# Behind the last store of a decoder layer: 46 ways of reading the streamed tokens on TensorE

## The chip, the cores and the metric

The kernel runs on one core of one Trainium2 chip. The time is device microseconds of that core for one execution of the whole program; a run's median is compared with the median of the kernel before on the same chip. The profile is of one execution, and its span runs from the first to the last recorded instruction.

## The reference

One layer of a hybrid decoder is computed for 256 prompt tokens and 8 sample tokens (264 in all) of width 2048, in float32:

```python
def rmsnorm(x, g):
    xf = x.astype(jnp.float32)
    y = xf * lax.rsqrt(jnp.mean(xf * xf, axis=-1, keepdims=True) + EPS)
    return (y * g.astype(jnp.float32)).astype(x.dtype)
...
    x = x + jnp.concatenate([y_rg, y_ml], axis=-1) @ w_out       # RG-LRU and mLSTM groups
...
    x = x + o @ w_xa_o                                           # cross-attention
    xf = rmsnorm(x, g_ffn)
    x = x + (jax.nn.silu(xf @ w_ffn_gate) * (xf @ w_ffn_up)) @ w_ffn_down
...
    y_prompt = rmsnorm(xp, g_final)
    y_sample = rmsnorm(xs, g_final)
```

The outputs are `y` of all tokens and the new states and memory keys and values.

## The kernel before

Activations are held transposed: features lie on the 128 partitions, tokens along the free dimension. So a product streams the 264 tokens as the moving operand of TensorE past 128x128 blocks of a weight matrix as the stationary one. Each float32 number is split into a rounded part and a rest, both in float32r, and `mm3` (line 232) multiplies with three matmuls: high by high, high by low, low by high.

The work is a list `steps`: each step loads one 128x2048 piece of a weight matrix from memory (two halves of 128x1024, tag `raw`), splits it with ScalarE and VectorE into tiles of the tag `w` (4 buffers of `WW` = 2176 columns), and runs its matmuls into one PSUM bank of `bank()` (line 288, tag `mm`, 4 buffers). Inside a `w` tile the blocks lie 264 columns apart from column 48 on (`wrows`, line 214). The tokens lie in tiles of `Arr` (line 121): four chunks of 264 tokens behind one another in a tile of `BW` = 1088 columns, from column 0 or, in every second tile, from column 32. All matmuls of the kernel stream such tokens, or weights, with a step of one column.

The order of the instructions on SyncE is the program's; the other engines' order comes from the scheduler of the framework, which simulates a timeline. Other work (recurrences, attention) is done by generators between the steps.

The end of the program: `final(m)` (line 930) takes the 16 pieces of the last product, adds them into `xres` and writes the scaled rows to `st["y"]`, four `Arr` tiles of four chunks each. After the last one `rstd_fin` (line 375) works out the reciprocal root of the mean square. A loop at the very end multiplies the 16 chunks of `st["y"]` in place (line 1344: chunks 4, 5, 10 and 11 on GpSimd, the others on VectorE) and stores them in 9 transfers to `o_y` from the queues of SyncE and ScalarE (line 1345). `warm(n)` (line 293) is a helper that runs matmuls into a bank that nobody reads.

Of the kernel before, what the change touches and what calls it, by code (L numbers as in the profile page):

```python
# [11 lines left out]
F32R = mybir.dt.float32r  # L12
I32 = mybir.dt.int32
AF = mybir.ActivationFunctionType
# [3 lines left out]
P = 128  # L18
# [4 lines left out]
N = T + NS  # L23
# [57 lines left out]
def layer_kernel(ctx: ExitStack, tc, xT, memT, vec, wrg, w_in, w_out, w_q, w_k, w_v, w_o,  # L81
                 w_gu, w_d0, w_d1, w_d2, c0T, kcT, vcT,
                 o_y, o_h, o_cp, o_cs, o_pc, o_sc, o_sn, o_m, o_k, o_v):
    nc = tc.nc
    act, dve, pe = Engine(nc.scalar, price_act), Engine(nc.vector, price_dve), Engine(nc.tensor, price_pe)
# [3 lines left out]
    sb = ctx.enter_context(tc.tile_pool(name="sb", bufs=1))  # L89
# [29 lines left out]
    WO, WW = 48, 8 * N + 64  # L119
# [119 lines left out]
    st = {}  # L239
# [18 lines left out]
    def side(g, prio=0):  # L258
        x = Gen(g, prio)
        gens.append(x)  # L260
        gens.sort(key=lambda q: q.prio)
        return x
# [43 lines left out]
    def V(name, j=0, w=1):  # L306
        o = _V[name][0] + j
        return vecs[:, o: o + w]
# [52 lines left out]
    def sumsq(acc, x, first):  # L361
        if first:
            return act.activation(acc, x, AF.Square)
        s = tmp(x.shape[-1])
        i = act.activation(s, x, AF.Square)
        dve.tensor_add(acc, acc, s)
        return i

    def split(h, l, x, g):

        act.activation(h, x, AF.Copy, scale=g)
        dve.scalar_tensor_tensor(l, x, g, h.bitcast(F32), op0=OP.mult, op1=OP.subtract)
# [536 lines left out]

    def residual(m, gname, key, last):

        def f(ps):
            x = xres[:, m, :]
            dve.tensor_add(x, x, ps[:, :N])
            if key is None:
                return
            if m == 0:
                st[key] = HL(KC)  # L920
            split(*st[key](m), x, V(gname, m))
            sumsq(acc_x, x, m == 0)
            if m == KC - 1:
                st["rstd_" + key] = side(last(), -1)
        return f
# [56 lines left out]
    for m in range(KC):  # L982
        proj(w_out[m], ry, residual(m, "g_xa", "xa", norm_x),
             need=("rgout",) if m == 0 else ())
# [23 lines left out]
    pairs = []  # L1008
# [213 lines left out]
    def evac_xo(m):  # L1222
        f = residual(m, "g_ffn", "ffn", norm_x)

        def g(ps):
            if m == 0:
                return
            if m == 1:
                residual(0, "g_ffn", "ffn", norm_x)(held[0][0])
            f(ps)  # L1230
        return g
# [109 lines left out]
    for lo, hi in ((0, 1), (1, 2), (2, 4), (4, 6), (6, 8), (8, 10), (10, 12), (12, 14), (14, 16)):  # L1341
# [2 lines left out]
            e.tensor_mul(st["y"](c), st["y"](c), r)  # L1344
        (act if lo in (1, 4, 8, 12) else sp).dma_start(o_y[:, lo:hi, :], st["y"].tile(lo // 4)[:, lo % 4: lo % 4 + hi - lo, :])


# [1 line left out]
_OUTS = [("o_y", (P, KC, N)), ("o_h", (P, RGB, 1 + NS)), ("o_cp", (P, RGB, 3)), ("o_cs", (P, RGB, NS, 3)),  # L1349
# [102 lines left out]
```

## Time and profile before

| what | value |
|---|---|
| median of 2 runs | 1552.89 us |
| the 2 runs | 1550.15 and 1555.63 us |
| span of the profiled execution | 1548.1 us |
| busy TensorE matmuls | 1533.5 us, 12098 records |
| busy weight loads | 1500.4 us, 12098 records |
| busy VectorE, ScalarE, GpSimd | 1055.5, 784.0, 123.7 us |
| mean granted TensorE clock | 0.997 |

The page gives no total time of the profiled execution beside its span of 1548.1 us; the two runs lie 2.0 and 7.5 us above that span. Times are from the span's start. The recorded length of a matmul includes its way through the pipeline, so matmuls overlap in the records: their rate is read from a count over a stretch of time, not from the length of one.

### The profile page before, as it was taken

Reading aid. Unit: us, or ns where it says so; the run is one execution under the profiler, and the core shown is the slowest. Engines: PE = TensorE matmul, PEld = TensorE weight load, DVE = VectorE, ACT = ScalarE, POOL = GpSimd, SP = SyncE. Lnnn points to the kernel's source line nnn. Section 1 sums busy time; section 2 is a strip of 40 time slices with the busy share of each in tenths; the row PEclk is TensorE's granted clock in tenths of the full one; section 3 lists DMA queues with packets and bytes.
Section 4 is the critical chain, followed back from the end, with each engine's and each line's share of the span. In section 5 each row is a group of like instructions: output and inputs, shape, how many; then the busy total and the mean of one; then the engine's idle time right before and its main releaser. Section 6 shows DMA issues by size and latency. Waiting matters only on the chain.

```text
span 1548.1 us, 30188 instructions
## 1 busy us (share of the span) xinstructions
PE 1533.5 (99%) x12098; PEld 1500.4 (97%) x12098; DVE 1055.5 (68%) x2026; ACT 784.0 (51%) x1255; POOL 123.7 (8%) x190
## 2 busy tenths in 40 slices
PE   9999999999999999999999999999999999999997
PEld 9999999999999888899999999999999999999997
DVE  7886888796699989876665555445555545555554
ACT  7565775665455656555444444333444433444463
POOL 0001210000134333310000000000000000000000
PEclk9999999999999999999999999999999999999999
DMA  9556984547789887855555555555555555555563
GB/s 301 187 164 204 309 288 171 193 158 259 251 294 356 320 296 252 309 181 180 187 177 181 186 181 188 181 185 183 183 185 181 186 183 186 180 188 178 163 181 107
DMA packets 99757, 326.01 MB, mean 211 GB/s; under 512 B 10945, under 2 KB 19825, under 8 KB 99617
## 3 DMA queue, kind: packets, MB, share of 16 engines
q1 hardware_dynamic: 83472, 269.57, 52.1%
q0 software_dynamic: 15136, 53.16, 9.7%
q8 instruction: 94, 1.54, 0.4%
q10 hardware_dynamic: 1008, 1.36, 0.3%
q14 instruction: 47, 0.38, 0.1%
HBM read 312.78 MB, written 11.28 MB: 209 GB/s over the span
## 4 chain that ended last, share of the span: by engine, by line
PE 96%; DVE 2%; ACT 1%; DMA 0%; issue 0%; SPq 0%; DVEq 0%; ACTq 0%
PE mm L60 90%; PE ax L60 6%; DVE B L60 1%; ACT B L60 0%; DVE w L60 0%; DMA raw<-w_in 0%; ACT w L60 0%; ACT L60 0%; DVE xres L60 0%; DVE c L60 0%; ACT rstd L60 0%; SPq L1278 0%; DVE acc_x L60 0%; DVEq L1429 0%; ACT t L60 0%
## 5 line engine op out<-in xcount | busy, mean ns | idle before, releaser
L60 PE MATMUL mm<-B,w 128*128 128x264 f32 (+1 forms) x10960 | 1365.3, 285 | 4.1 <-DVE w L60 2.4
L60 PEld LDWEIGHTS mm<-B,w 128*128 128x128 f32 x10960 | 1338.6, 188 | 16.4 <-DVE w L60 2.8
L60 ACT ACTIVATE w<-raw 128x1024 fp32r<-128x1024 f32 (+1 forms) x522 | 537.9, 1031 | 654.6 <-PE mm L60 447.3
L60 DVE TENSOR_TENSOR w<-raw,w 128x1024 fp32r<-128x1024 f32 (+1 forms) x522 | 623.1, 1195 | 357.0 <-ACT w L60 356.0
L60 PE MATMUL mm<-w,B 128*128 128x512 f32 x384 | 91.0, 391 | 0.0
L60 PEld LDWEIGHTS mm<-w,B 128*128 128x128 f32 x384 | 70.7, 188 | 14.3
L60 DVE TENSOR_TENSOR t<-mm,rstd 128x264 f32<-128x264 f32 x104 | 44.8, 431 | 44.2 <-PE mm L60 43.5
L1344 POOL TENSOR_TENSOR B<-B,rstd 128x264 f32<-128x264 f32 x4 | 2.8, 736 | 855.5 <-ACT rstd L60 855.5
L60 DVE TENSOR_TENSOR xres<-xres,mm 128x264 f32<-128x264 f32 (+1 forms) x81 | 34.2, 423 | 38.9 <-PE mm L60 38.9
L60 DVE SCALAR_TENSOR_TENSOR B<-B,dw 128x256 f32<-128x256 f32 x128 | 55.6, 488 | 3.9 <-ACT dw L60 3.9
L60 DVE SCALAR_TENSOR_TENSOR dw<-B,qsm,dw 128x256 f32<-128x256 f32 x96 | 49.6, 525 | 0.4
L60 PE MATMUL ax<-B,B 128*128 128x256 f32 (+3 forms) x288 | 48.1, 308 | 0.0
L60 PEld LDWEIGHTS ax<-B,B 128*128 128x128 f32 x288 | 40.8, 190 | 3.2 <-ACT w L60 0.3
L1031 POOL TENSOR_TENSOR ds<-dw,ds 128x256 fp32r<-128x256 f32 x32 | 34.6, 1085 | 108.1 <-ACT ds L60 108.1
L60 ACT ACTIVATE B<-xres,vecs 128x264 fp32r<-128x264 f32 (+1 forms) x64 | 32.1, 502 | 1.5 <-DVE xres L60 1.0
L60 ACT ACTIVATE t<-xres 128x264 f32<-128x264 f32 (+2 forms) x61 | 24.0, 410 | 15.2 <-DVE xres L60 15.2
L1020 POOL DMA_DIRECT2D B<-kcT x32 | 17.3, 542 | 140.1 <-DVE B L60 131.0
L60 ACT ACTIVATE B<-t 128x264 fp32r<-128x264 f32 (+1 forms) x60 | 24.2, 409 | 4.6 <-DVE t L60 4.3
L60 DVE TENSOR_TENSOR acc_x<-acc_x,t 128x264 f32<-128x264 f32 x59 | 25.1, 426 | 1.0 <-ACT t L60 0.5
L60 DVE SCALAR_TENSOR_TENSOR B<-xres,vecs,B 128x264 fp32r<-128x264 f32 x48 | 23.4, 487 | 3.1 <-ACT B L60 3.1
L60 ACT ACTIVATE t<-t 128x264 f32<-128x264 f32 (+1 forms) x61 | 24.8, 406 | 1.3 <-DVE t L60 1.2
L60 ACT ACTIVATE dw<-B,qsm 128x256 f32<-128x256 f32 x32 | 16.2, 507 | 17.4 <-DVE B L60 10.7
(152 smaller groups left out, 666.9 us busy)
## 6 DMA issues: line engine op xcount, KB each, us to landing
raw<-w_gu SPq DMA_DIRECT2D x176, 512.0 KB, 3.5
raw<-w_d SPq DMA_DIRECT2D x80, 512.0 KB, 3.5
raw<-w_in SPq DMA_DIRECT2D x74, 512.0 KB, 4.6
raw<-w_out SPq DMA_DIRECT2D x32, 512.0 KB, 4.0
B<-kcT POOLq DMA_DIRECT2D x32, 512.0 KB, 8.1
raw<-w_q SPq DMA_DIRECT2D x32, 512.0 KB, 3.7
B<-vcT POOLq DMA_DIRECT2D x32, 512.0 KB, 8.5
raw<-w_k SPq DMA_DIRECT2D x32, 512.0 KB, 6.8
```

Of the source, the lines that this page charges most:

```text
L60: return f(*a, **k)
L1020: pool_e.dma_start(kc, kcT[h, b])
L1031: pool_e.tensor_sub(ws[:, 1], acc, ws[:, 0].bitcast(F32))
L1344: e.tensor_mul(st["y"](c), st["y"](c), r)
```

## The change

A function `probes` is called after the loop with the last stores. It takes three tiles of the tag `w` and has ScalarE fill them with copies of tiles 0, 1 and 2 of `st["y"]` (six copies of 1056 columns, three of 64). Then 46 access patterns follow, each with 24 matmuls: the stationary operand is a block of 128 columns of the first tile, taken in turn from 8 places 264 columns apart; the moving operand is the pattern's view of the second tile, in float32r. The 24 matmuls add up in one bank; the output is written to columns that lie next to one another, whatever the pattern. Nothing reads the bank, and the third tile isn't read either. TensorE's order in this part is the program's.

A pattern is a start column and a list of [step, count], the outermost first. So "pairs 132 apart" streams columns 0, 132, 1, 133, 2, ..., and "step 4" streams 0, 4, 8, ... 37 patterns have 264 columns, eight have 256, one 248.

```diff
+    def probes(y):
+        RL = 24
+        wt = [sb.tile([P, WW], F32R, tag="w", bufs=4, name=nm("w")) for _ in range(3)]
+        for n, t in enumerate(wt):
+            for q in range(2):
+                act.activation(t[:, q * 1056: q * 1056 + 1056].rearrange("p (c n) -> p c n", n=N), y.tile(q + n % 2), AF.Copy)
+            act.activation(t[:, 2112:2176], y.tile(n)[:, 0, 0:64], AF.Copy)
+        banks = [bank() for _ in range(2)]
+        mm = nc.tensor.matmul
+        W_ = lambda k: wt[0][:, 264 * (k % 8): 264 * (k % 8) + P]
+        with tc.manual_schedule(engines={mybir.EngineType.PE}):
+            pat = [
+                ("plain", 0, [[1, 264]]), ("plain", 0, [[1, 264]]),
+                ("step 2", 0, [[2, 264]]), ("step 3", 0, [[3, 264]]), ("step 4", 0, [[4, 264]]), ("step 5", 0, [[5, 264]]),
+                ("step 6", 0, [[6, 264]]), ("step 7", 0, [[7, 264]]), ("step 8", 0, [[8, 264]]),
+                ("pairs 132 apart", 0, [[1, 132], [132, 2]]), ("pairs 16 apart", 0, [[1, 132], [16, 2]]),
+                ("pairs 32 apart", 0, [[1, 132], [32, 2]]), ("pairs 64 apart", 0, [[1, 132], [64, 2]]),
+                ("pairs 264 apart", 0, [[1, 132], [264, 2]]), ("pairs 1024 apart", 0, [[1, 132], [1024, 2]]),
+                ("pairs 2 apart", 0, [[1, 132], [2, 2]]), ("pairs 8 apart", 0, [[1, 132], [8, 2]]),
+                ("fours 66 apart", 0, [[1, 66], [66, 4]]), ("fours 264 apart", 0, [[1, 66], [264, 4]]),
+                ("fours 16 apart", 0, [[1, 66], [16, 4]]), ("eights 33 apart", 0, [[1, 33], [33, 8]]),
+                ("eights 264 apart", 0, [[1, 33], [264, 8]]), ("twelves 22 apart", 0, [[1, 22], [22, 12]]),
+                ("pairs of pairs", 0, [[2, 66], [132, 2], [1, 2]]), ("fours in turn", 0, [[4, 33], [132, 2], [1, 4]]),
+                ("eights in turn", 0, [[8, 16], [128, 2], [1, 8]]), ("sixteens in turn", 0, [[16, 8], [128, 2], [1, 16]]),
+                ("each twice", 0, [[1, 132], [0, 2]]), ("each four times", 0, [[1, 66], [0, 4]]),
+                ("halves twice", 0, [[0, 2], [1, 132]]), ("sixteen again and again", 0, [[0, 16], [1, 16]]),
+                ("eight again and again", 0, [[0, 33], [1, 8]]), ("two again and again", 0, [[0, 132], [1, 2]]),
+                ("sixty-four again", 0, [[0, 4], [1, 64]]), ("four again and again", 0, [[0, 66], [1, 4]]),
+                ("backward lines", 255, [[-16, 16], [1, 16]]), ("backward in lines", 15, [[16, 16], [-1, 16]]),
+                ("backward", 263, [[-1, 264]]),
+                ("start 4", 4, [[1, 264]]), ("start 8", 8, [[1, 264]]), ("start 12", 12, [[1, 264]]), ("start 1", 1, [[1, 264]]),
+                ("256 columns", 0, [[1, 256]]), ("256 from 8", 8, [[1, 256]]), ("248 columns", 0, [[1, 248]]), ("plain", 0, [[1, 264]]),
+            ]
+            for name, o, ap in pat:
...
+                for k in range(RL):
+                    mm(out, W_(k), x, start=k == 0, stop=k == RL - 1, skip_group_check=True)
...
+    probes(st["y"])
```

More of the change, by code (lines that the diff above doesn't have):

```diff
@@ L907, in layer_kernel @@
         proj(w_in[33 + j], rx, evac_o(j))
+    def probes(y):
[32 more added lines that the diff above has]
+            for name, o, ap in pat:
+                n = int(np.prod([q[1] for q in ap]))
+                src = wt[1][:, o: o + 1]
+                x = bass.AP(src.tensor, src.offset, [list(src.ap[0])] + [list(q) for q in ap])
+                out = banks[0][:, :n]
+                if len(ap) == 2:
+                    out = out.rearrange("p (a b) -> p a b", a=ap[0][1])
+                if len(ap) == 3:
+                    out = out.rearrange("p (a b c) -> p a b c", a=ap[0][1], b=ap[1][1])
+                for k in range(RL):
+                    mm(out, W_(k), x, start=k == 0, stop=k == RL - 1, skip_group_check=True)
```

## The prediction

> **What bounds the kernel now.** I read the shares of busy time first, then the chain that ended last, then the windows, and last the timeline of the final ten microseconds, because the change sits there.
>
> ```profile
> span 1548.1 us, 30188 instructions
> PE 1533.5 (99%) x12098; PEld 1500.4 (97%) x12098; DVE 1055.5 (68%) x2026; ACT 784.0 (51%) x1255; POOL 123.7 (8%) x190
> ...
> PE 96%; DVE 2%; ACT 1%; DMA 0%; issue 0%; SPq 0%; DVEq 0%; ACTq 0%
> ```
>
> TensorE is the bound, 96% of the chain by its matmuls. So the time is a count of matmuls times what one takes in a dense stream. Recorded lengths (282 ns) overlap, so I take that from a count over a stretch: the windows (columns: the stretch, its length, then busy time and count of PE, PEld, DVE, ACT, POOL, then granted clock, DMA share, GB/s), and the group of the same stretch.
>
> ```profile
> core 0: us, PE busy (x) PEld busy (x) DVE busy (x) ACT busy (x) POOL busy (x), PEclk, DMA share, GB/s
> 1000.00:1500.00 500.00, 500.00 (x4178) 500.00 (x4177) 272.89 (x329) 209.64 (x250) 0.00 (x0) 1.00 0.55 181
> 1500.00:1535.00 35.00, 35.00 (x295) 35.00 (x294) 18.38 (x30) 17.43 (x29) 0.00 (x0) 1.00 0.37 111
> ...
> 1541.00:1544.00 3.00, 0.00 (x0) 0.00 (x0) 2.27 (x7) 0.00 (x0) 2.10 (x3) 0.71 0.95 360
> 1544.00:1548.00 4.00, 0.00 (x0) 0.00 (x0) 0.00 (x0) 0.00 (x0) 0.00 (x0) 0.50 0.59 223
> ```
> ```profile
> L60 PE MATMUL mm<-B,w 128*128 128x264 f32 x4178 | 500.4, 282 | 0.0
> ```
>
> All 4178 matmuls of that stretch stream 264 columns, one step apart, with new weights for each: 500 / 4178 = **119.7 ns**. With the transfers lighter (111 instead of 181 GB/s) it is 35 / 295 = 118.6 ns. In both the weight loads are as dense as the matmuls.
>
> The end of the program, in the timeline:
>
> ```profile
> 1538.24 1.41 PEld L60 LDWEIGHTS ax<-ident,c 128*128 128x128 f32 x12 [0.29 <-DVE c L60]
> 1538.24 1.50 PE L60 MATMUL ax<-ident,c 128*128 128x128 f32 x12
> 1539.12 4.16 DVE L60 TENSOR_TENSOR B<-B,ax 128x264 f32<-128x264 f32 x12 [0.93 <-PE ax L60]
> 1539.57 4.73 SPq L1345 DMA_DIRECT2D o_y<-B  x5
> 1539.78 0.39 ACT L60 ACTIVATE rstd<-ax 128x264 f32<-128x264 f32 x1 [2.39 <-PE ax L60]
> 1539.92 3.21 ACTq L1345 DMA_DIRECT2D o_y<-B  x4
> 1540.26 2.84 POOL L1344 TENSOR_TENSOR B<-B,rstd 128x264 f32<-128x264 f32 x4 [855.47 <-ACT rstd L60]
> ```
>
> TensorE ends at 1538.24 + 1.50 = 1539.74 us. VectorE's multiplications end at 1543.28, GpSimd's at 1543.10, ScalarE's last store is issued by 1543.13, SyncE's by 1544.30. The windows show the granted clock falling to 0.71 and 0.50 once TensorE idles.
>
> **The change part by part.** It removes nothing and moves nothing: the probes read the finished `y`, so no matmul of them can run earlier, and every one lies on the path that sets the end, with no other work beside it. Six parts add up.
>
> *When the probes can start.* The first matmul needs parts of two copied tiles, made by ScalarE from tiles 0, 1 and 2 of `y`. Their price is the nearest copy:
>
> ```profile
> L60 ACT ACTIVATE w<-raw 128x1024 fp32r<-128x1024 f32 x6 | 6.4, 1059 | 4.8 <-ACT B L60 4.8
> ...
> L60 ACT ACTIVATE c<-c 128x3 f32<-128x3 f32 x1 | 0.2, 204 | 0.5 <-DVE c L60 0.5
> ```
>
> A copy of 1056 columns is put at 1.06 us and one of 64 at 0.25 us, so the first two tiles cost 2 x (2.12 + 0.25) = 4.7 us of ScalarE. If all of that follows its last store issue (1543.13), it ends at 1547.9; if the scheduler slips copies into the waits between those issues, the first matmul can go at about 1543.5. I take **1546.0**, with 1543.5 to 1548 as bounds. The third tile is copied beside the matmuls and costs nothing; without that cover it would be 2.4 us. A store issue that a copy delays by 1 us is covered too, by 180 us of matmuls.
>
> *The cold clock.* TensorE has then idled for 6 us, at a clock of 0.50. What such a stretch costs shows earlier in the run:
>
> ```profile
> 122.00:126.00 4.00, 4.00 (x23) 4.00 (x22) 4.00 (x6) 0.61 (x2) 0.00 (x0) 0.57 0.59 180
> 126.00:130.00 4.00, 4.00 (x35) 4.00 (x35) 3.14 (x12) 2.70 (x4) 1.08 (x2) 1.00 0.96 309
> ```
>
> At 0.57 it started 12 matmuls fewer in 4 us: 12 x 0.12 = **1.4 us**. Twice that is the upper bound, if the clock comes back one such stretch later.
>
> *The patterns in which neighbours in the stream are neighbours in the tile.* No row shows a step other than one, so the cost is bounded. The lower end for any pattern is 119.7 ns. The upper end comes from the weight loads and from a stream taken twice:
>
> ```profile
> 62.96 1.05 PE L60 MATMUL ax<-B,B 128*128 128x264 f32 x4
> ```
> ```profile
> L60 PE MATMUL ax<-B,B 128*128 128x264 f32 x32 | 8.4, 386 | 0.0
> ```
> ```profile
> L60 PEld LDWEIGHTS ax<-ident,c 128*128 128x128 f32 x64 | 7.7, 190 | 0.3 <-DVE c L60 0.3
> ```
>
> A float32 record of 264 columns starts every (1.05 - 0.386) / 3 = 0.221 us, 1.85 times the float32r one. Weight loads alone, twelve in 1.41 us, start every (1.41 - 0.19) / 11 = 0.111 us for 128 columns: 0.87 ns a column, against 119.7 / 264 = 0.45 ns for the stream. So the stream takes two columns in the time in which the weight side takes one. My estimate is that the stream fetches neighbours together, two at least, and that a column without its neighbour costs a fetch of its own: 264 x 0.867 = **229 ns**, which is also nearest to the 221 ns row. That is a choice between the ends, not something this trace shows.
>
> By that I sort the 46 patterns. In 18 every two successive columns lie four or more columns apart: steps 4 to 8 (5), pairs 132, 16, 32, 64, 264, 1024 and 8 apart (7), the fours (3), eights 33 and 264 apart (2), twelves (1). "Step 3" I put halfway: (119.7 + 229) / 2 = 174 ns. The other 27 (plain, step 2, pairs of pairs, repeats, backward, other starts, fewer columns) are put at 119.7 ns; their unknowns are "start 1", "pairs 2 apart" and "backward lines", where pairs may be cut (+55 ns each, 4 us in all), and "248 columns", up to the 221 ns row (+2.4 us).
>
> [...]
>
> *The sum of the streams.* 18 x 24 x 0.229 = 98.9 us; 24 x 0.174 = 4.2 us; 27 x 24 x 0.1197 = 77.6 us. Together **180.7 us** for 1104 matmuls.
>
> *A different place of the weights.* The kernel's own weights start at column 48 of their tile, the probes' at 0. Whether the two reads meet differently can't be read off; the widest streams of the run, at another place again, cost 91.0 / 384 = 237 ns for 512 columns, 0.463 ns a column, 2% above 0.453. I take nothing, and allow up to +11 us (10 ns a matmul) or -8 us (7 ns, to the 112 ns at which weight loads bound).
>
> ```profile
> L60 PE MATMUL mm<-w,B 128*128 128x512 f32 x384 | 91.0, 391 | 0.0
> ```
>
> *What follows the last matmul.* About 0.3 us until it ends, then what now follows the last landing:
>
> ```profile
> L1345 SPq DMA_DIRECT2D o_y<-B x5: 332/344/755, 1539.6 to 1543.5; - x5
> ...
> DMA to landing us min/median/max: 1.8/2.3/3.3
> ```
>
> The last store is issued at 1543.5 and landed by 1546.8 at the latest, so **1.3 us** of closing follow it. The stores are hidden behind the probes.
>
> The sum: 1546.0 + 1.4 + 180.7 + 0.3 + 1.3 = 1729.7 us of span, 181.6 above 1548.1. The page gives no total beside the span; the two runs (1550.15 and 1555.63) lie 2.0 and 7.5 us above it, so the profiled execution stands within 5 us of either, and I add the difference to the median: 1552.89 + 181.6 = 1734.5, **1734 us**.
>
> **The rivals.**
>
> *Every pattern streams at the plain rate.* 46 x 24 x 0.1197 = 132.2 us, 48.5 less: **1686 us**. For it: in the trace the time of a matmul follows its columns alone (264 and 512 within 2%). Against it: none of those streams has a step. [...]
>
> *Only wide steps pay.* If a fetched neighbourhood is kept for some accesses, the interleaved patterns (13 of the 18) come back to it in time, and only steps 4 to 8 and half of "step 3" pay: 132.2 + 5 x 24 x 0.109 + 24 x 0.055 = 146.6 us, so **1700 us**. For it: the pairs use up all neighbours, merely in turns. Against it: it needs a store of several neighbourhoods, of which no row tells.
>
> *A lone column costs four.* If the plain stream lives on four neighbours a fetch and the fetches are at their limit, a lone column takes 4 x 0.453 = 1.8 ns: 478 ns a matmul, 18 x 24 x 0.478 = 206.5, "step 3" (three fetches for four columns) 8.6, the rest 77.6, in all 292.7: **1846 us**. Against it: weight loads run beside the plain stream at nearly their own pace (0.111 to 0.120 us), so fetches have room.
>
> *The matmuls are left out*, since nobody reads their bank: then only the copies stay, ending at 1543.1 + 7.1 = 1550.2, or 1551.5 with the closing: **1556 us**, not slower. It decides if 30 records and more like them are missing. Against it: `warm` is just as unread, and its matmuls ran.
>
> ```profile
> L60 PE MATMUL mm<-ones 128*128 128x128 f32 x30 | 6.2, 393 | 1.1 <-DVE ones L60 1.1
> ```
>
> **How the numbers follow.** The forecast, lone columns at 221 to 250 ns, has a chance of 0.56, with its own range from 1720 (start 2.5 us earlier, 8 us from the weights' place, 3.5 us at 221 ns) to 1762 (+2 start, +1.4 clock, +11 place, +6.4 open patterns, +9 at 250 ns, minus what rarely comes together). The plain rate everywhere has 0.15, only wide steps 0.12, four times 0.11, left out 0.02; 0.04 is for sizes between. The range from **1682 to 1790** holds the forecast, the plain rate and the wide steps, and leaves out four times, left out and some of the rest: 0.15 to 0.17. A measurement of this kernel can tell about 2%, or 31 us, from no change. All cases but the left-out one add over 130 us: slower 0.97, within 2% 0.02, faster 0.01.
>
> **What would show it.** In the changed profile: 1104 more matmuls after 1540 us; the first 24 (plain) starting at about 0.22 us until the clock is granted, the next 24 near 120 ns; "step 2" like plain; "step 4" and every pair but "2 apart" at 229 ns; the three plain groups equal apart from the clock; no change before 1539 us. A "step 4" at 120 ns, pairs at 120 ns beside steps at 229, or any pattern near 480 ns would prove the forecast wrong in that order of the rivals; a first matmul after 1549 us would break the first term.

## The result and the profile after

The changed kernel takes **1713.93 us** (1713.47 and 1714.40), 161.0 us more than before; the ratio is **1.1043**, with a 95% interval from 1.1022 to 1.1064. The forecast was 1734 us, 12% too much for what the probes add. The patterns were sorted wrongly, and the total is as near as it is because errors of both signs met in the sum: about 26 us too much, about 7 too little.

The page after:

```profile
span 1712.6 us, 32407 instructions
PE 1698.4 (99%) x13202; PEld 1658.4 (97%) x13202; DVE 1056.3 (62%) x2026; ACT 790.5 (46%) x1264; POOL 123.6 (7%) x190
...
PE mm L60 80%; PE mm L958 10%; PE ax L60 5%; DVE B L60 1%; ACT B L60 1%; DVE w L60 0%; DMA B<-scr 0%; ACT w L60 0%; DMA raw<-w_in 0%; DMA o_sc<-B 0%; DMA scr<-lt 0%; ACT L60 0%; POOL B L792 0%; DVE t L60 0%; ACTq L1479 0%
...
L958 PE MATMUL mm<-w,w 128*128 128x264 f32 (+2 forms) x1104 | 163.6, 316 | 5.5 <-ACT w L60 5.5
```

TensorE has 13202 records, 1104 more, and line 958 (the probes' matmul) holds 163.6 us and 10% of the chain. How they began, in the timeline:

```profile
1540.73 1.50 PE L60 MATMUL ax<-ident,c 128*128 128x128 f32 x12
...
1543.09 1.23 ACT L60 ACTIVATE w<-B 128x1056 fp32r<-128x1056 f32 x2 [0.42 <-DVE B L60]
1544.22 1.39 ACTq L1393 DMA_DIRECT2D o_y<-B  x3
1545.65 5.12 ACT L60 ACTIVATE w<-B 128x1056 fp32r<-128x1056 f32 x6 [1.34 <-POOL B L1392]
```

The scheduler did slip copies between ScalarE's store issues; the rest followed them. What each kind of pattern cost stands in the windows, cut at the first matmul of a kind. Their counts include a few matmuls that only reach into a stretch, so a price is the length over 24 matmuls a pattern.

```profile
core 0: us, PE busy (x) PEld busy (x) DVE busy (x) ACT busy (x) POOL busy (x), PEclk, DMA share, GB/s
1547.76:1552.26 4.50, 4.50 (x24) 4.50 (x25) 0.00 (x0) 3.02 (x4) 0.00 (x0) 0.63 0.25 91
1552.26:1555.17 2.91, 2.91 (x27) 2.91 (x25) 0.00 (x0) 0.00 (x0) 0.00 (x0) 1.00 0.00 0
1555.17:1566.46 11.29, 11.29 (x51) 9.94 (x50) 0.00 (x0) 0.00 (x0) 0.00 (x0) 1.00 0.00 0
1566.46:1594.35 27.89, 27.89 (x121) 24.80 (x120) 0.00 (x0) 0.00 (x0) 0.00 (x0) 1.00 0.00 1
1594.35:1615.97 21.62, 21.62 (x194) 21.62 (x192) 0.00 (x0) 0.00 (x0) 0.00 (x0) 1.00 0.01 2
1615.97:1626.17 10.20, 10.20 (x74) 10.20 (x73) 0.00 (x0) 0.00 (x0) 0.00 (x0) 1.00 0.00 0
1626.17:1643.01 16.84, 16.84 (x74) 14.98 (x73) 0.00 (x0) 0.00 (x0) 0.00 (x0) 1.00 0.00 1
1643.01:1647.11 4.10, 4.10 (x26) 4.10 (x24) 0.00 (x0) 0.00 (x0) 0.00 (x0) 1.00 0.00 0
1647.11:1711.09 63.98, 63.98 (x528) 63.98 (x528) 0.00 (x0) 0.00 (x0) 0.00 (x0) 1.00 0.00 1
```

| stretch | patterns | ns a matmul | forecast |
|---|---|---|---|
| 1547.76 | plain, cold (clock 0.63) | 188 | 178 |
| 1552.26 | plain | 121 | 119.7 |
| 1555.17 | step 2 and step 3 | 235 | 119.7 and 174 |
| 1566.46 | steps 4 to 8 | 232 | 229 |
| 1594.35 | all 8 pairs | **112.6** | 229 (one of them 119.7) |
| 1615.97 | three fours | 142 | 229 |
| 1626.17 | two eights, twelves | 234 | 229 |
| 1643.01 | pairs of pairs | 171 | 119.7 |
| 1647.11 | the other 22 | 121 | 119.7 |

So interleaving columns that lie 16 or 1024 apart is not slow: at 112.5 ns each it is 8 ns faster than streaming them one after another. And a step of 2 (236 ns) is as slow as one of 8 (225). The 22 of the last row are not alike: "each twice" and "each four times" take 112.5 ns, "start 1" 125, "backward in lines" 133 and "backward lines" 148.

### The profile page after: what moved, and what is told of

Its sections match the earlier page's. It is cut to its first block, busy times and chain, and to the rows that moved or that the text cites. A ratio compares the mean times of both kernels' runs of the same rounds, so it can differ in the third digit from the quotient of the medians.

```text
span 1712.6 us, 32407 instructions
## 1 busy us (share of the span) xinstructions
PE 1698.4 (99%) x13202; PEld 1658.4 (97%) x13202; DVE 1056.3 (62%) x2026; ACT 790.5 (46%) x1264; POOL 123.6 (7%) x190
## 4 chain that ended last, share of the span: by engine, by line
PE 94%; DVE 2%; DMA 1%; ACT 1%; issue 1%; POOL 0%; ACTq 0%; DVEq 0%; SPq 0%; POOLq 0%
PE mm L60 80%; PE mm L958 10%; PE ax L60 5%; DVE B L60 1%; ACT B L60 1%; DVE w L60 0%; DMA B<-scr 0%; ACT w L60 0%; DMA raw<-w_in 0%; DMA o_sc<-B 0%; DMA scr<-lt 0%; ACT L60 0%; POOL B L792 0%; DVE t L60 0%; ACTq L1479 0%
## 5 line engine op out<-in xcount | busy, mean ns | idle before, releaser
L958 PE MATMUL mm<-w,w 128*128 128x264 f32 (+2 forms) x1104 | 163.6, 316 | 5.5 <-ACT w L60 5.5
L958 PEld LDWEIGHTS mm<-w,w 128*128 128x128 f32 x1104 | 157.1, 195 | 11.9 <-ACT w L60 5.6
```

Of the source, the lines that this page charges most:

```text
L958: mm(out, W_(k), x, start=k == 0, stop=k == RL - 1, skip_group_check=True)
```

## The experiments

**All plain, and copies alone.** The two runs take the change apart: one makes every pattern "plain", the other leaves out the 1104 matmuls and keeps the copies. The edits, shortened:

```diff
-            pat = [ ("plain", 0, [[1, 264]]), ... 46 patterns ]
+            pat = [ ("plain", 0, [[1, 264]]) ] * 46            # e3
-                for k in range(RL):
+                for k in range(0):                             # e4
```

> All 46 patterns are 'plain', so 1104 matmuls of 264 columns with a step of one. The sum of the change's trace, if patterns cost what they show there and nothing else: 1104 x 0.121 = 133.6 us instead of 162.0, so 28 us less than the change: 1713.9 - 28 = 1685 us, 1.085 of before. If the patterns' prices are partly a change of state that outlasts them (a clock, a queue), the plain ones would be off 121 ns and the total off 1685 by more than 5 us.

> The three tiles are copied, and none of the 1104 matmuls is issued. The copies end on ScalarE about 4 to 7 us after the last store's issue, so 1553 to 1558 us, within 2% of before. The forecast's terms for the start, the cold clock and the closing would be left unchanged by it. If the added code by itself (scheduling, instruction fetch) slows the body, this would show as more than 1562 us.

Measured: all plain 1687.90 us, ratio 1.0874 (1.0856 to 1.0892); copies alone 1552.79 us, ratio 1.0008 (0.9999 to 1.0017). The copies and the code by itself cost no more than 3 us together, and perhaps nothing; 1552.79 lies just under the 1553 to 1558 that were expected. All plain is 26.0 us below the change; by the windows the change's streams took 163.3 us with the cold start, and 1104 plain ones at 121 ns with 1.6 us of cold start take 135.2, 28 us less. In the trace of all plain the streams take 136.7 us: the clock stood at 0.50 over the first 24 (5.44 us where the change's took 4.50), and from the third pattern on a matmul takes 121 ns to the end. That is 1.5 of the 3 us by which all plain missed its 1685; the rest is about the spread between its runs (1687.53 to 1688.91). So the patterns' prices add up, and they leave nothing behind.

**Words or shapes.** 50 other patterns in the place of the 46; the edit is shortened, as those that follow are. Each of the four runs with other patterns was executed once (1754.7, 1694.6, 1686.2 and 1620.2 us, in the order of this section), and their prices are read inside one trace, at a granted clock of 1.00.

```diff
-                ("step 2", 0, [[2, 264]]), ...
+                ("twos every 3", 0, [[3, 132], [1, 2]]), ("twos every 4", 0, [[4, 132], [1, 2]]), ...
+                ("fours every 8", 0, [[8, 66], [1, 4]]), ("fours every 8 from 1", 1, [[8, 66], [1, 4]]), ...
+                ("pairs 1056 apart step 2", 0, [[2, 132], [1056, 2]]), ("pairs 1056 apart step 4", 0, [[4, 132], [1056, 2]]), ...
+                ("six held", 0, [[0, 44], [44, 6]]), ("eight held", 0, [[0, 33], [33, 8]]), ...
```

> Another list of 50 patterns, 24 matmuls each, all else as in the change. Theory A, kept words: the stream fetches aligned words of two columns, one in about 0.87 ns, and keeps the last two to four of them; a word that is still kept is not fetched again. Theory B, shape: the time hangs on the count and the step of the innermost run alone (2 columns: 112 ns; 4: 142; a long run with a step: 230), whatever the addresses. 'Pairs 1056 apart step 2' and 'step 4', 'pairs 264 apart step 2' (runs of 2, no word used twice): A 230 ns, B 112. 'Step 2 in pairs': A 236, B 112. 'Step 2 each twice', 'step 8 each twice': both 112 to 121. 'Plain in pairs' (same columns as plain, written as runs of 2): A 121, B 112. 'Twos every 4 from 1' and 'from 3' (each two cut a word): A 230, B 112; from 0 and 2: A 121, B 112; with words of four columns instead of two, 'from 1' would be 121 and only 'from 3' 230. 'Four held' and 'two held': A 112; 'eight held', eight columns repeated in turn, far apart: A 230 if fewer than eight words are kept, 'six held' between; B 142 for four, about 230 for eight. 'Eight held 2 apart' (8 words in a row): A as 'eight held'. 'Turned fours' (0, 2, 1, 3, 4, 6, ...): A 112, B 112. 'Sixes 44 apart': both between 142 and 231. The run as a whole: 20 to 60 us over the change's 40 patterns, no theory hangs on it.

The windows of that run, in this order: plain in pairs, fours and eights together with plain (four patterns); twos every 3; twos every 4; fours every 8 and every 16; fours every 8 from 1 and from 2; step 8 each twice; pairs 1056 apart with step 2; with step 4; six held; eight held.

```profile
1557.23:1568.86 11.63, 11.63 (x98) 11.63 (x97) 0.00 (x0) 0.00 (x0) 0.00 (x0) 1.00 0.00 0
1568.86:1573.12 4.26, 4.26 (x26) 4.26 (x25) 0.00 (x0) 0.00 (x0) 0.00 (x0) 1.00 0.02 4
1573.12:1578.76 5.64, 5.64 (x25) 4.97 (x25) 0.00 (x0) 0.00 (x0) 0.00 (x0) 1.00 0.00 0
...
1618.45:1624.31 5.86, 5.86 (x49) 5.86 (x48) 0.00 (x0) 0.00 (x0) 0.00 (x0) 1.00 0.01 3
1624.31:1635.61 11.30, 11.30 (x51) 9.97 (x49) 0.00 (x0) 0.00 (x0) 0.00 (x0) 1.00 0.00 0
...
1638.53:1644.27 5.74, 5.74 (x26) 4.99 (x25) 0.00 (x0) 0.00 (x0) 0.00 (x0) 1.00 0.00 0
1647.19:1650.01 2.82, 2.82 (x26) 2.82 (x25) 0.00 (x0) 0.00 (x0) 0.00 (x0) 1.00 0.02 6
1650.01:1655.65 5.64, 5.64 (x26) 4.96 (x25) 0.00 (x0) 0.00 (x0) 0.00 (x0) 1.00 0.00 0
...
1729.22:1732.02 2.80, 2.80 (x26) 2.80 (x25) 0.00 (x0) 0.00 (x0) 0.00 (x0) 1.00 0.00 0
1732.02:1737.38 5.36, 5.36 (x27) 4.93 (x26) 0.00 (x0) 0.00 (x0) 0.00 (x0) 1.00 0.00 0
```

Both theories fall. Shape is out: the same columns written as pairs, fours or eights cost the same 121 ns, and runs of two cost 117.5 ns (pairs 1056 apart, step 2) or 235 (step 4), by their addresses. Words of two columns are out as well: "twos every 4" uses whole words of two and costs 235 ns. In two patterns both theories agreed and both were wrong: "step 8 each twice" costs 239 ns (expected 112 to 121), "turned fours" 121 (112). What fits is a count of **aligned fours of columns** (0 to 3, 4 to 7 and so on from the tile's column 0), called lines here: fours every 8 cost 122 ns from column 0, and 235 from column 1 or 2, where each four is cut by a line's end. "Twos every 3" (178 ns) lies between, as three of four of its pairs touch a new line. And six columns far apart, repeated in turn, cost 117 ns, eight cost 223, as if about three lines a position stayed open and four did not.

That gives theory E, an estimate from these prices, with one price of its own: the stream is taken two columns at a time, and a pair that opens a line takes 1.82 ns (240 ns for the 132 pairs of "step 4"), while 264 columns take at least 112.5 ns, the lowest that a pattern of the change took. Lines, openings and hiding are the theory's words for what it counts; the traces show the time of each pattern, not what TensorE does in it. In its count plain opens a line with every second pair: 66 x 1.82 = 120 ns, just over its 112.5. Pairs 132 apart open two lines at once and then use them for three more pairs: 33 openings, 60 ns, hidden behind 112.5.

**Other sides.** The same probes with the weights taken from other places, and with other column counts.

```diff
-                W_ = lambda k: wt[0][:, 264 * (k % 8): 264 * (k % 8) + P]
+                # a pattern may name (first column, pitch, places, tile) of its weights, as
+                ("plain, weights at 48", 0, [[1, 264]], {"w": (48, 264, 8, 0)}), ("plain, weights 128 apart", 0, [[1, 264]], {"w": (0, 128, 8, 0)}),
+                ("512 plain", 0, [[1, 512]]), ("512 pairs", 0, [[1, 256], [256, 2]]), ("512 step 2", 0, [[2, 512]]), ...
```

> 38 patterns with the weights taken from other places and with other column counts. Theory C, the two reads meet: the 121 ns of plain against the 112.5 of the pairs is the stream's fetches colliding with the weight loads; then plain moves between 112 and 135 ns with the place of the weights (column 48, 2, 8, 16, 32, 128 or 256 apart, one place only, the same tile), and 'pairs' stays at 112.5 with each of them. Theory D, a fixed cost of a switch of weights: plain is 120 to 122 ns with every place of the weights, and only the pattern moves it. Column counts: '512 plain' 227 ns (as the kernel's own), '512 pairs' 216 if the gain is one of 8 ns or more a matmul, 'turned fours of 512' the same; '128 plain' and '128 pairs' both 112, since the weight load of 128 columns bounds them; '512 step 2' and '512 step 4' 445 to 465 ns if the price is one fetch per column; '128 step 2' 112 to 120. 'Turned fours' with weights at 48, from 32, 128 apart: 112.5 by both.

The windows: twelve plain patterns with the weights in twelve places; four pairs patterns, weights in four places; 512 plain; 512 pairs; 512 step 2.

```profile
1556.42:1591.27 34.85, 34.85 (x290) 34.85 (x289) 0.00 (x0) 0.00 (x0) 0.00 (x0) 1.00 0.00 1
1591.27:1602.07 10.80, 10.80 (x98) 10.80 (x97) 0.00 (x0) 0.00 (x0) 0.00 (x0) 1.00 0.01 2
...
1604.89:1610.50 5.61, 5.61 (x26) 4.51 (x25) 0.00 (x0) 0.00 (x0) 0.00 (x0) 1.00 0.00 0
1610.50:1615.68 5.18, 5.18 (x25) 4.53 (x24) 0.00 (x0) 0.00 (x0) 0.00 (x0) 1.00 0.00 0
1623.66:1634.55 10.89, 10.89 (x27) 5.02 (x27) 0.00 (x0) 0.00 (x0) 0.00 (x0) 1.00 0.00 0
```

The place of the weights hardly counts, as theory D had it: 34.85 / 288 = 121.0 ns over the twelve, each between 120.0 and 121.8, and 10.80 / 96 = 112.5 for pairs in all four. So theory C falls. D falls too, as its cost is a fixed one for each switch of weights: the gain of pairs grows with the columns, 8.5 ns at 264 and 5.61 to 5.18 us over 24, or 233.9 to 215.8 = 18 ns, at 512. 512 plain was expected at 227 ns; 128 lines x 1.82 = 233 ns is theory E's price. "Turned fours", expected at 112.5 ns with 264 columns and 216 with 512, take 121 to 122 and 233.9, as plain does: in theory E they open as many lines as plain. 512 step 2 is 454 ns. With 128 columns plain and pairs are both 110 to 112 ns, as the weight loads alone take (0.111 us in the prediction).

**Theory E put to the test**, with 37 patterns whose openings were counted ahead.

```diff
+                ("turned eights", 0, [[8, 33], [1, 4], [4, 2]]), ("fours every 5", 0, [[5, 66], [1, 4]]), ("fours every 6", 0, [[6, 66], [1, 4]]),
+                ("fours every 7", 0, [[7, 66], [1, 4]]), ("sixes every 8", 0, [[8, 44], [1, 6]]), ("eights every 12 from 2", 2, [[12, 33], [1, 8]]),
+                ("six held in twos", 0, [[0, 44], [4, 3], [1, 2]]), ("pairs 134 apart", 0, [[1, 132], [134, 2]]), ...
```

> Theory E, opening pairs: the stream is taken two columns at a time; a pair that touches a line of four columns (16 bytes, aligned) which the pair before it did not touch opens it, and such a pair takes 1.82 ns; a matmul takes the larger of 112.5 ns (264 columns) and 1.82 ns x its opening pairs. Counted for new patterns: 'turned eights' (0, 4, 1, 5, 2, 6, 3, 7) 33 opening pairs, 112.5 ns, the same with weights at 48 and start 32; of 512 columns 216, of 256 109 to 112; 'fours every 5' 83 pairs, 151 ns; 'fours every 6' 99, 180; 'fours every 7' 98, 178; 'sixes every 8' from 0, 1 and 2, 88 each, 160; 'eights every 12' 120 from 0, but 180 from 1 and from 2; 'twos every 4 twice' 120 and 'three times' 112.5; 'pairs 4 apart every 8 twice' 120; 'twos every 5' and 'pairs 2 apart every 4' 240; 'start 1' to 'start 3' 120 to 124; 'pairs 132 apart from 1' 112.5; 'pairs 134 apart' 120 (its two lines change in different pairs). Rival F, words of two columns kept in a small store: 'fours every 6' 121, 'sixes every 8' 121, 'eights every 12 from 2' 121, 'twos every 5' from 121 to 180. What theory E leaves open is how many lines stay open: 'six held in twos' (3 lines), 'eight held in twos' (4), 'twelve again' (3), 'six held 2 apart' (3): 112 to 117 if three lines stay, 240 (120 for 'twelve again') if only the last pair's.

The windows: turned eights in two places; fours every 5; every 6; every 7; sixes every 8 from 0, 1 and 2; eights every 12 from 2 and from 1; eight held in twos; six held in twos; pairs 134 apart.

```profile
1556.72:1562.12 5.40, 5.40 (x51) 5.40 (x49) 0.00 (x0) 0.00 (x0) 0.00 (x0) 1.00 0.00 0
...
1586.95:1590.54 3.59, 3.59 (x26) 3.59 (x24) 0.00 (x0) 0.00 (x0) 0.00 (x0) 1.00 0.00 0
1590.54:1594.83 4.29, 4.29 (x26) 4.29 (x25) 0.00 (x0) 0.00 (x0) 0.00 (x0) 1.00 0.00 0
1594.83:1599.24 4.41, 4.41 (x25) 4.41 (x25) 0.00 (x0) 0.00 (x0) 0.00 (x0) 1.00 0.00 0
1599.24:1610.58 11.34, 11.34 (x74) 11.34 (x73) 0.00 (x0) 0.00 (x0) 0.00 (x0) 1.00 0.01 1
...
1613.50:1621.96 8.46, 8.46 (x51) 8.46 (x49) 0.00 (x0) 0.00 (x0) 0.00 (x0) 1.00 0.00 0
1647.43:1653.15 5.72, 5.72 (x25) 5.01 (x24) 0.00 (x0) 0.00 (x0) 0.00 (x0) 1.00 0.01 3
1653.15:1655.97 2.82, 2.82 (x25) 2.81 (x24) 0.00 (x0) 0.00 (x0) 0.00 (x0) 1.00 0.00 0
1677.38:1680.08 2.70, 2.70 (x26) 2.70 (x25) 0.00 (x0) 0.00 (x0) 0.00 (x0) 1.00 0.00 0
```

In order: 112.5 ns (expected 112.5), 150 (151), 179 (180), 184 (178), 157.5 (160), 176 (180); rival F's 121 is out. Four lines repeated in turn cost 238 ns, near the 240 of an opening in every pair; three cost 117.5, near the 112 to 117 expected if three stay. These four lines are used at both positions of the pairs; the six columns of "six held" lie on six lines, three at each position, and cost 117 ns. So a count of six lines kept for both positions together does not fit. One miss: "pairs 134 apart" took 112.5 ns, not 120. Its two positions change lines in different pairs, and yet the price is that of one change. That would fit if the odd and the even positions of the stream, two lanes, opened lines each for itself, side by side.

**Lanes and runs of openings** put that to the test, and the patterns above that theory E does not price: fours (142 ns) and pairs of pairs (171), where openings follow one another directly.

```diff
+                ("pairs 3 apart", 0, [[1, 132], [3, 2]]), ("pairs 130 apart", 0, [[1, 132], [130, 2]]), ("pairs 133 apart step 2", 0, [[2, 132], [133, 2]]), ...
+                ("twos of fours 16 apart", 0, [[16, 33], [0, 2], [4, 4]]), ("twos of sixes", 0, [[24, 22], [0, 2], [4, 6]]), ...
```

> Two refinements of theory E, each against its plainer form. Lanes: the odd and the even positions of the stream are two lanes that fetch for themselves, and a matmul takes the larger of the column time and 1.82 ns x the lines opened in the busier lane, three lines staying open in each; against pairs, where the two positions open together. 'Pairs 3, 5, 6, 7, 130, 131 apart' (the two lanes change lines in different pairs): lanes 112.5 ns, pairs 120. 'Pairs 133 and 134 apart step 2': lanes 120, pairs 236. Runs of openings: m openings that follow one another in a lane, before h positions without one, take m x 1.82 + h x 0.85 ns if m is 2 or more, only a lone one being hidden; against full hiding, where the larger of 1.82 x openings and the column time stands. 'Twos of fours' (0, 4, 8, 12, 0, 4, 8, 12, 16, ...; m 2, h 2): 176 against 120. 'Threes of fours' (2, 4): 155 against 112.5. 'Fives of fours' (2, 8; 260 columns): 136 against 111. 'Twos of sixes' (3, 3): 176 against 120. 'Threes of sixes' (3, 6; 252 columns): 148 against 108. 'Threes of twos' (1, 2): 112.5 by both. 'Sixes 44 and 264 apart step 2' (3, 3): 176 against 120. 'Twos of eights' (four lines a lane, so none stays): 233 by both.

The windows: pairs 3, 5, 6, 7, 130 and 131 apart; twos of fours; twos of sixes; pairs 133 and 134 apart with step 2.

```profile
1555.05:1571.27 16.22, 16.22 (x146) 16.22 (x145) 0.00 (x0) 0.00 (x0) 0.00 (x0) 1.00 0.01 1
1571.27:1575.28 4.01, 4.01 (x27) 4.01 (x26) 0.00 (x0) 0.00 (x0) 0.00 (x0) 1.00 0.00 0
1582.01:1586.81 4.80, 4.80 (x27) 4.80 (x25) 0.00 (x0) 0.00 (x0) 0.00 (x0) 1.00 0.00 0
1608.22:1614.14 5.92, 5.92 (x49) 5.92 (x49) 0.00 (x0) 0.00 (x0) 0.00 (x0) 1.00 0.00 0
```

The count by lanes holds: 112.6 ns for the six, 123 for the two with step 2 (pairs would be 120 and 236). It goes by the position and not by the column: "pairs 134 apart step 2", one of the two at 123, streams even columns alone. For runs of openings full hiding does not fit, that much is shown: twos of fours take 167 ns where it gives 120. The formula for them is only near: 167 (176), 148 (155) and 132 (136) for runs of two, 200 (176), 159 (148), 200 and 188 (176) for runs of three. Their size stays open.

**The kernel itself with another order.** The body's 10 thousand matmuls stream plain, at 120 ns; by theory E this is the price of the line openings, above the 112.5 ns that the pairs took for 264 columns. So two versions of the kernel before, without probes, stream every eight tokens as 0, 4, 1, 5, 2, 6, 3, 7, and VectorE reads the bank back in token order: k1 in the gate, up and down products, k2 in 10560 of the 10624 of 264 columns (there ScalarE scales the keys in an instruction of its own).

```diff
+    def turned(x):
+        return x.rearrange("p (g b a) -> p g a b", b=2, a=4)
+    def streamed(ps):
+        return ps.rearrange("p (g a b) -> p g a b", a=4, b=2)
+    def nat(ps):
+        return ps.rearrange("p (g a b) -> p g b a", a=4, b=2)
+    def el(x):
+        return x.rearrange("p (g b a) -> p g b a", b=2, a=4)
+    def mm3t(ps, a, b, start, stop):
+        ah, al = a
+        bh, bl = (turned(x) for x in b)
+        ps = streamed(ps)
...
-            dve.tensor_mul(b, ps[:, :N], rstd)
+            dve.tensor_mul(el(b), nat(ps[:, :N]), el(rstd))
```

> The kernel before, without probes. In the gate, up and down products (6336 of the matmuls with 264 columns) the tokens are streamed as 0, 4, 1, 5, 2, 6, 3, 7 of every eight, and VectorE reads the bank back in the order of the tokens. Theory E: 112.5 instead of 119.7 ns in that part, 6336 x 7.2 = 46 us less: 1506 us, 0.970 of before. If the gain of the probes is only that of an idle core (no transfers, no other engines), or VectorE's reads at a step of two hold TensorE up: 1540 to 1560 us.

> The same in all products of 264 columns made with three matmuls (some 10500 matmuls). Theory E with nothing else in the way: 10500 x 7.2 = 76 us less: 1476 us, 0.951 of before. Before 700 us VectorE is 76 to 90% busy in many slices and TensorE waits more often there; if these waits take the gain of that part, only that of the part after 650 us is left (some 7000 matmuls): 1500 us. Slower than before only if VectorE's reads of the bank cost more than about twice as much.

Measured: k1 **1506.40 us**, ratio 0.9708 (0.9694 to 0.9723); k2 **1482.81 us**, ratio 0.9557 (0.9541 to 0.9573). The first window is of k1, then a group of k1 and the same group of before in the same stretch:

```profile
1000.00:1400.00 400.00, 400.00 (x3558) 400.00 (x3557) 232.61 (x272) 172.62 (x200) 0.00 (x0) 1.00 0.56 196
```
```profile
L60 DVE TENSOR_TENSOR t<-mm,rstd 128x264 f32<-128x264 f32 x51 | 22.1, 433 | 17.3 <-PE mm L60 17.3
```
```profile
L60 DVE TENSOR_TENSOR t<-mm,rstd 128x264 f32<-128x264 f32 x44 | 19.0, 432 | 22.4 <-PE mm L60 22.4
```

400 / 3558 = 112.4 ns a matmul, with transfers at 196 GB/s and the other engines at work, against 119.7 before; VectorE's read of the turned bank costs 433 ns against 432. k1 gains 45.3 us where 46 were expected. k2 gains 68.9 of 76; TensorE's listed waits add up to 11.5 us there against 6.2 before, which would be 5 of the missing 7. Both beat the kernel before, so the gain is not one of an idle core alone, which would have left k1 at 1540 to 1560 us.

## Why the prediction was right, and where it was not

The direction was right, and so were all terms but one, within 2.5 us. The mechanism of that one was not: by the prediction's own signs, pairs near 120 ns beside steps at 229 mean that the forecast fails in favour of "only wide steps pay", and 112.6 beside 232 came. The time lies below the forecast's own range (1720 to 1762) and nearer to that rival's 1700 than to 1734. Only the wide range, 1682 to 1790, which was built to hold the rivals too, holds it.

The span grew by 164.5 us (1712.6 - 1548.1), forecast 181.6. By its terms:

- *The start of the probes* was forecast 6.3 us after TensorE's last matmul and came after 5.5 (1547.76 - 1542.23): right, and for the reason given, copies partly slipped between the store issues.
- *The cold clock*: 4.50 us for the first 24 plain matmuls, at a granted clock of 0.63, against 2.91 for the second at 1.00, 1.6 us; forecast 1.4. Right.
- *The closing*: 1.5 us from the last matmul's start to the end of the span; forecast 1.6. Right.
- *Nothing else moves*: TensorE's last matmul of the body ended 2.5 us later than in the trace of before. The run of the copies alone speaks against the added code (1.0008). In the changed kernel's profiled execution the clock stayed at half for longer near 122 us (0.50 and then 0.78 below, where the rows of before in the prediction have 0.57 and 1.00), which is a part of it; why it did is open.

```profile
122.00:126.00 4.00, 4.00 (x20) 4.00 (x20) 4.00 (x6) 0.71 (x2) 0.00 (x0) 0.50 0.58 178
126.00:130.00 4.00, 4.00 (x28) 4.00 (x28) 3.34 (x12) 1.67 (x3) 0.96 (x2) 0.78 0.90 287
```

- *The sum of the streams* is the term that failed: 180.7 us forecast, 161.7 measured (163.3 less the cold 1.6). The failed step is the sorting: "a column without its neighbour costs a fetch of its own". The size of the price was right, 229 ns against 225 to 240 for steps 4 to 8, but by luck as far as the runs show: it was taken from the weight loads (0.867 ns a column), and what fits the prices is 1.82 ns for a line in each of two lanes. Seven of the 18 patterns, the pairs, took 112.5 ns (19.6 us too much in the sum), and the fours 142 (6.3 us too much); theory E puts this down to lines that stay open for their other columns. And steps 2 and 3 and the pairs of pairs took 236, 235 and 171 (5.5 us too little together); in its count steps 2 and 3 have a new line at every position of a lane, and pairs of pairs openings in direct succession. The distance of neighbours fits none of these prices. In the other patterns 1.5 us too little was forecast. "Only wide steps pay" had half of it: the pairs cost what kept neighbourhoods would cost, but the eights took 227 and 231 ns.
- *A different place of the weights*: nothing taken, and over twelve places plain stays between 120.0 and 121.8 ns. Right. The 237 ns that the prediction read for 512 columns are too many, as busy time holds the end of each group's last matmul too: in the trace of before 65 of them go by in 14.76 us (650.63 to 665.39), 227 ns each, 0.443 ns a column. So these streams are not 2% dearer by the column than those of 264 but 2% cheaper; the forecast took nothing from them, only a bound.
- *The rivals*: "the plain rate everywhere" is out, and with it the reading that a matmul's time is its columns alone: the trace of the change shows 112.5 to 243.5 ns for the same 264. Nor does it settle the price that a line is used twice: step 2 has two columns on each and takes 236 ns, "step 8 each twice" two in a row and 239. And two columns in turn from different lines cost the pairs nothing (112.6 ns). What fits is the count within a lane. "A lone column costs four" is out too: the dearest pattern of the change's trace, the twelves, took 243.5 ns and not 478.

The span of the run profiled after lies 1.8 us under its time (1714.40), so the trace of before, at 1548.1, belongs near the quicker of its two runs; that is why 164.5 us of span are 161.0 us between the medians.

## What to carry to other kernels

The price of a stream was estimated from the weight loads beside it, and the range was kept wide enough for the rivals; so the range held although the sorting was wrong, and a total within its range proves no term. A matmul that runs a few per cent slower than its columns take at best (here (215.8 - 112.5) / (512 - 264) = 0.417 ns each) is worth a probe with the columns in another order: here 120 against 112.5 ns pointed to a version that is 4.4% faster than the kernel it was measured on. Before a layout is changed for locality, count the fours of columns that its stream changes to, at odd and at even positions: here the count gave the price of 40 of 45 patterns of the change within 7%, and missed the fours (142 ns against 112.5), where two changes follow one another.

## What the runs showed of the hardware

- Prices of streams in float32r at a granted clock of 1.00: 264 plain columns 120.0 to 121.8 ns, 512 plain 233.9; turned eights 112.5 and 215.8; any step from 2 to 8, 225 to 240; six columns far apart repeated in turn 117, eight 223.
- Theory E with lanes is an estimate from such prices: 1.82 ns (240 / 132) for each change to another aligned four of columns, counted for the odd and the even positions apart, three fours that stay open in each (117 ns against 223), and a lone change hidden where the columns take longer (112.5 ns). No trace shows the lines or the lanes themselves. Why a lane of 132 lines takes 223 in one pattern and 243 in another stays open.
- In the trace of the change, without the first, cold pattern, the larger of the column time (112.5 ns for 264) and 1.82 ns x the busier lane's lines comes within 7% of the measured time for 40 of 45. Four of the other five are slower and have two openings in direct succession: the fours (142 ns against 112.5) and the pairs of pairs (171 against 120). "Backward in lines" is slower (133 ns against 117) for a reason that no run shows. The price comes from this trace itself. Elsewhere "eight held" is faster (223 against 240), and the patterns of the run on lanes with two or three openings in direct succession took 132 to 200 ns where it gives 107 to 120. In the theory E run, for which the openings were counted ahead, the windows above hold ten patterns from "turned eights" to "eights every 12" that took within 4% of the expected times, and "pairs 134 apart", which took 112.5 ns where 120 were expected; the lanes came after it.
- The order of the stream cost VectorE nothing when it read the bank at a step of two (433 against 432 ns).
